# Slot counts of the experts in a two-layer backbone with routed experts: 44 and 44 quarters become 43 and 41

## The chip, the cores and the metric

The kernel runs on one core of a Trainium2 chip. The metric is the device time of one execution in microseconds (us). TensorE (PE) multiplies, VectorE (DVE) and ScalarE (ACT) work on its results, GpSimd (POOL) issues the gathers and stores of the expert layers, and SyncE (SP) issues the loads of weights. All transfers run on the core's 16 DMA engines.

## The reference, cut to what matters

512 tokens of width 1024 pass two layers. Each layer has a mixer (windowed attention in the first, a gated MLP over chunks in the second), a layer norm, and a mixture of 16 experts of which each token uses two; then another layer norm. All is float32.

```
def routed_moe(h, router_w, router_bias, w1, w3, w2):
    s = sigmoid(h @ router_w); s_sel = s + router_bias
    # of 4 groups of 4 experts the best group, of it the best two experts
    gate = sc / sum(sc)
    # for each expert, for its tokens:
    y = (silu(x @ w1[e]) * (x @ w3[e])) @ w2[e]
    out[token] += gate * y
```

An expert's w1 and w3 are 1024 x 512 each, its w2 is 512 x 1024. The number of tokens that an expert gets follows from the data: 1024 choices are spread over 16 experts.

## The kernel before, in words

**Slots.** The number of rows for an expert is fixed when the program is built. `VIS` (L29) lists for each layer 16 visits in the order in which they are done, as (rank, slots). Rank 0 is the expert that got the most tokens, 13 the one that got the fewest, among experts 0 to 13; experts 14 and 15 have rank -1 and come first, because their weights can be loaded before the routing is known. A token beyond the slots of its expert goes to a block for overflow (`more`), which runs only where a count needs it. Slots come in quarters of 32 rows. The first layer has 44 quarters, the second too.

**Units and groups.** `units_of` (L38) lays the visits' slots one behind the other in rows, in groups of 128 rows, and cuts them into units of 128, 64 or 32 rows that don't cross a group's edge. A layer has 11 groups: the rows of a group are gathered together from `hdr` by one indirect transfer on POOL's queue (`gather`, L994) and transposed on PE (`to_xT`, L1003). The list of a group's tokens comes from one-hot rows that DVE makes, one operation for each visit in the group and each of four blocks of tokens (`slots`, L977), and small matmuls (`tokens`, L960). The lists of group 0 and of groups 1 to 3 are made before the loop, those of the others in it.

**A unit's work.** `gemm1` (L1029) multiplies the unit's rows with w1 and w3: 8 weights of 128x1024, for 64 and 32 rows in 2 and 4 parts that lie side by side in the array. `glu` (L1040) is one operation on ACT and one on DVE, `to_hT` (L1049) transposes on PE and copies on ACT, `gemm2` (L1062) multiplies with 4 weights, `store` (L1072) scales on DVE and writes to `ydr` on POOL's queue, one transfer for 128 rows, two for 64, four for 32. In the loop of `moe` (from L1162) the second product of a unit comes after the first product of the next one. A float32 matmul stands as two instructions in the trace.

**Weights.** Each visit needs 12 pieces of 512 KB, all visits of a layer but the first two 168. `moe_pieces` (L162) puts them in order: eight for a visit's first product, and a visit's last four behind the first eight of the next, where it has one unit. SP issues them (L221) into a ring of tiles in a pool of 28 slots (NS); a piece that takes the slot of an older one waits until the last unit of that visit has used it. The expert of rank 0 in the second layer has 320 slots, in five units before the change, and holds its weights until the fifth.

**The end of a layer.** The last two units stay on the chip; the results of the others are gathered from `ydr` (`collect`, L1101), for which POOL waits until the last store has landed, and added to x on DVE (L1114). `last_norm` (L674) multiplies the last two units with their one-hot rows (L688), adds them (L696) and norms.

The order on each engine is set by a scheduler at build time, from the program's order and its dependencies.

Of the kernel before, what the change touches and what calls it, by code (L numbers as in the profile page):

```python
# [18 lines left out]
D = 1024  # L19
T = 512  # L20
NT = 4
E = 16
# [3 lines left out]
LOOK = 25  # L26


VIS = ([(-1, 64), (-1, 64), (4, 96), (0, 128), (8, 64), (5, 96), (6, 96), (9, 64), (7, 96), (1, 128), (10, 64), (11, 64),  # L29
# [3 lines left out]

NOV = 10
NR = E - 2
# [1 line left out]

def units_of(l):  # L38

    r, row = [], NOV * 128  # L40
    for v, (_, cap) in enumerate(VIS[l]):
        o = 0
        while o < cap:
            left = min(cap - o, 128 - row % 128)
            n = max(m for m in (128, 64, 32) if m <= left)
            r.append((v, o, n, row))
            o, row = o + n, row + n
    assert row % 128 == 0 and [u[2] for u in r[-2:]] == [64, 64]
    return r, row


UNITS = [units_of(l)[0] for l in range(2)]

ZR = [units_of(l)[1] - 128 for l in range(2)]


# [4 lines left out]
def make_consts():  # L61
# [26 lines left out]
    for l in range(2):  # L88
# [3 lines left out]
        cap, base = np.zeros(E), np.zeros(E)  # L92
        for v, (r, n) in enumerate(VIS[l]):
            k = NR + v if r < 0 else r
# [7 lines left out]
def hybrid_kernel(ctx: ExitStack, tc: tile.TileContext, A, out):  # L102
    nc = tc.nc
    V, SC, PE, GP, SP = nc.vector, nc.scalar, nc.tensor, nc.gpsimd, nc.sync
# [14 lines left out]
    def slot(shape, dt=F32, nm="s"):  # L119
        return S.tile(shape, dt, name=f"{nm}{nid()}", tag="s")  # L120
# [25 lines left out]
    def tt2(shape, dt=F32, nm="t"):  # L146
        return sm.tile(shape, dt, name=f"{nm}_{nid()}", tag="t2", bufs=9)
# [43 lines left out]
    def issue(n):  # L191
        while issued[0] < min(n, limit[0]):
            p = pieces[issued[0]]
            if p[0] == "moe" and p[2] > 1:
                raws[p] = slot([128, 1024], F32, "ring")
                fetch(p[1], VIS[p[1]][p[2]][0], p[3], raws[p])
                issued[0] += 1
# [18 lines left out]
    def fetch(l, r, j, t):  # L216

        if (l, r) not in regs:
            regs[l, r] = nc.values_load(RT[l]["int"][0:1, r:r + 1], engines=[mybir.EngineType.SP], min_val=0,
                                        max_val=E - 1, skip_runtime_bounds_check_because=why)  # L220
        SP.dma_start(t, A["moe"][l, bass.ds(regs[l, r], 1), j].rearrange("a p n -> (a p) n"))  # L221
# [40 lines left out]
    zero = cst.tile([128, 128], F32, name="zero")  # L262
# [55 lines left out]
    ydr = dr.tile([max(ZR) + 1, D], F32, name="ydr")  # L318
    for z in ZR:
        SP.dma_start(ydr[z:z + 1, :].rearrange("o (a b) -> (o a) b", b=128), zero[0:8, :])  # L320

# [428 lines left out]
    NG = [ZR[l] // 128 + 1 - NOV for l in range(2)]  # L750
# [100 lines left out]
    def plan(l):  # L851
# [86 lines left out]
        def gates():  # L938
# [14 lines left out]
            for u in range(2):  # L953
                q = tt2([128, 4, NR], F32, "pq")
                r = VIS[l][u - 2][0]
                V.tensor_tensor(q, g[:, :, :NR], pm[:, None, r, :].to_broadcast([128, 4, NR]), op=OP.mult)
# [3 lines left out]
    def tokens(gi, hot, n):  # L960

        p = psB()
        for i in range(n):
            for t in range(4):
                oh = small([128, 128], BF, "oh", 6)
                hot(oh, i, t)
                PE.matmul(p[:, i * 4:i * 4 + 4], oh, aux[:, t, :], start=(i == 0 and t == 0), stop=(t == 3),
                          skip_group_check=True)
        r = small([128, NOV, 4], F32, "sr")[:, :n]
        V.tensor_copy(r.rearrange("p a b -> p (a b)"), p[:, :n * 4])  # L970
        ix = small([128, NOV], F32, "six")[:, :n]
        iv = small([128, NOV], F32, "siv")[:, :n]
        V.scalar_tensor_tensor(ix, r[:, :, 1], 128.0, r[:, :, 0], op0=OP.mult, op1=OP.add)
        V.tensor_scalar(iv, r[:, :, 2], -OOB, OOB, op0=OP.mult, op1=OP.add)
        return V.tensor_add(gi, ix, iv)

    def slots(l, g0, g1):  # L977
        R = RT[l]

        def hot(oh, i, t):  # L980
            r0 = (NOV + g0 + i) * 128
            for v, (r, cap) in enumerate(VIS[l]):
                a = next(row for w, o, n, row in UNITS[l] if w == v)
                c0, c1 = max(a, r0), min(a + cap, r0 + 128)
                if c0 < c1:
                    k = R["key"][:, t, NR + v:NR + v + 1] if r < 0 else R["kr"][:, t, r:r + 1]
                    V.tensor_scalar(oh[:, c0 - r0:c1 - r0], iotab[:, :c1 - c0], k, -float(c0 - a), op0=OP.subtract,
                                    op1=OP.is_equal)
        return tokens(R["gi"][:, g0:g1], hot, g1 - g0)
# [39 lines left out]
    def gemm1(n, xt, c, get, adv):  # L1029
        p = psA() if n == 128 else psB()  # L1030
        to = parts(n, p)
        for k in range(8):
            w = get(k).rearrange("p (m h c) -> p h m c", m=2, h=len(to))
            for h, o in enumerate(to):
                PE.matmul(o.rearrange("p (m c) -> p m c", m=2), xt[:, k, c:c + n], w[:, h], start=(k == 0), stop=(k == 7),  # L1035
                          skip_group_check=True)
            adv()
        return p if n == 128 else p[:, :n * 8]
# [42 lines left out]
    def last_slots(l):  # L1081
# [5 lines left out]
        for u in range(2):  # L1087
            pt = psT()
            k = VIS[l][u - 2][0]
            for t in range(4):  # L1090
# [25 lines left out]
    def moe(l, rest, X):  # L1116
        R = RT[l]
        gfr = mdr[l * 4 + 3:l * 4 + 4, :]
        gf = {128: load_row(gfr, alloc=xslot)}
        gs = xslot([128, 768], F32, "gfs")  # L1120
        gf[64], gf[32] = gs[:, :512], gs[:, 512:]
        for n in (64, 32):
            for h in range(128 // n):
                SC.dma_start(gf[n][h * n:h * n + n, :], gfr[:, h * n * 8:(h + 1) * n * 8].to_broadcast([n, n * 8]))
        xg = {}
        slots(l, 0, 1)
        xg[0] = gather(R["gi"][:, 0:1])
        places, rows, gates = plan(l)
        places()
        listed = slots(l, 1, 4)  # L1130
        for g in (1, 2):
            xg[g] = gather(R["gi"][:, g:g + 1])
        first = pos["moe", l, 0, 0]
        limit[0] = len(pieces) if l else pos["ws",]
        done = [0]
        units = UNITS[l]
        n = len(units)
        more(l, gf)
        xt = {0: to_xT(l, xg[0])}
        pend = None  # L1140

        def stage(i):
            v = units[i][0]
            lastuse = i + 1 == n or units[i + 1][0] != v

            def adv():
                if lastuse:
                    done[0] += 1
                    issue(first + done[0] + LOOK)
            return lambda j: raw("moe", l, v, j), adv  # L1150

        def fin():
            i, ht = pend
            py = gemm2(units[i][2], ht, *stage(i))
            if i < n - 2:
                store(units[i][2], units[i][3], py, gf)
            elif i == n - 2:
                R["yp"] = slot([128, 512], F32, "ys")
                V.scalar_tensor_tensor(R["yp"], py, R["gs"][:, 0:1], gf[64], op0=OP.mult, op1=OP.mult)
            return py  # L1160

        for i, (v, o, m, row) in enumerate(units):  # L1162
            g, c = row // 128 - NOV, row % 128
            p = gemm1(m, xt[g], c, *stage(i))
            s = glu(m, p)
            if i == 0:
                with tc.issue_after(rows().ins):
                    rest(0, 4)
            if c == 0 and 2 < g + 2 < NG[l]:
                xg[g + 2] = gather(R["gi"][:, g + 2:g + 3])  # L1170
            if c + m == 128 and g + 1 < NG[l]:
                if g:
                    xt[g + 1] = to_xT(l, xg[g + 1])
                else:
                    with tc.issue_after(listed.ins):
                        xt[g + 1] = to_xT(l, xg[g + 1])
                if g and g + 3 < NG[l]:
                    slots(l, g + 3, g + 4)
            if i == n // 2:
                gates()  # L1180
            if i == n - 4:
                last_slots(l)
            if pend:
                fin()
            if i == n - 2:
                collect(l, 1, uslot)
                collect(l, 0, slot)
            if i == n - 1:
                combine(l, 1, X)
            pend = (i, to_hT(m, s))  # L1190
        py = fin()
        combine(l, 0, X)
        limit[0] = len(pieces) if l else pos["moe", 1, 2, 0]
        return py, gf[64]
# [188 lines left out]
    p = psA()  # L1383
# [9 lines left out]
    for f in range(8):  # L1393
        wh, wl = hl("winu", f)
        p = psB()
# [10 lines left out]
        p = psT()  # L1406
# [83 lines left out]
```

## Time and profile before

| what | value |
|---|---|
| median of 3 runs | 1202.01 us (1195.79 to 1202.34) |
| profiled execution | 1199.04 us, span 1197.3 us |
| PE busy | 1032.2 us, 86% |
| DVE, ACT, POOL busy | 614.7, 360.4, 264.4 us |
| DMA | 330.98 MB, 276 GB/s on the mean |
| first expert layer, PE | about 391 to 652 us |
| second expert layer, PE | about 889 to 1157 us |

The profile is of one execution. Times in the trace count from the start of its span, which is 1.7 us shorter than the execution. A busy PE is one with matmuls in its pipeline; the ends of matmuls are modelled, so that a row's start is surer than its end.

### The profile page before, as it was taken

To read this page: it belongs to the slowest core of one execution; us is meant where nothing else is said; L and a number is where in the kernel's file an instruction comes from. 1 tells how busy PE (TensorE), PEld (TensorE's weight loads), DVE (VectorE), ACT (ScalarE), POOL (GpSimd) and SP (SyncE) were. 2 spreads that over 40 slices of the span, in tenths; PEclk is the share of its full clock that TensorE was granted. 3 is DMA by queue.
4 is the path that set the end of the run, shared out by engine and by line. 5 is a ranking of instruction groups with operands and counts; after the bars stand their busy time and mean duration, and the time that the engine had idled before them with its cause. 6 is when DMAs were issued, how large, how long until landed. Compare 5 with 4: busy or idle time off the path is not lost. (4 is left out here: it accounts for less than half of the span.)

```text
span 1197.3 us, 17660 instructions
## 1 busy us (share of the span) xinstructions
PE 1032.2 (86%) x6216; PEld 588.8 (49%) x6216; DVE 614.7 (51%) x1532; ACT 360.4 (30%) x726; POOL 264.4 (22%) x245
## 2 busy tenths in 40 slices
PE   6789899996992999999999499699749999999980
PEld 2567665553782344444443277588623444433430
DVE  1798999785357621211113987875655211221137
ACT  1553487775312111111111443451211111111103
POOL 0153343323000123231003253300010222211131
PEclk9898999997996999999999699799869999999995
DMA  9935457447274999999998126466559994999981
GB/s 341 404 138 183 151 207 245 167 148 250 90 264 171 372 406 390 410 410 409 410 408 314 78 105 212 141 214 222 211 189 411 410 410 172 377 410 409 410 317 70
DMA packets 103673, 330.98 MB, mean 276 GB/s; under 512 B 13057, under 2 KB 23761, under 8 KB 103570
## 3 DMA queue, kind: packets, MB, share of 16 engines
q1 hardware_dynamic: 88336, 287.43, 63.0%
q0 software_dynamic: 10512, 27.28, 6.0%
q10 hardware_dynamic: 4722, 14.98, 3.5%
q8 instruction: 54, 0.88, 0.3%
q14 instruction: 49, 0.40, 0.1%
HBM read 310.72 MB, written 22.07 MB: 278 GB/s over the span
## 5 line engine op out<-in xcount | busy, mean ns | idle before, releaser
L1035 PE MATMUL pb<-ring,xt 128*32 128x256 f32 (+1 forms) x1824 | 221.7, 461 | 0.3 <-DMA ring<-in_moe 0.2
L1035 PEld LDWEIGHTS pb<-ring,xt 128*32 128x32 f32 (+1 forms) x1824 | 81.6, 120 | 114.5 <-issue 80.7
L1079 POOL DMA_DIRECT2D ydr<-ys x114 | 58.3, 517 | 320.9 <-DVE ys L1074 240.0
L1046 DVE TENSOR_TENSOR si<-si,pb 128x256 f32<-128x256 f32 (+1 forms) x43 | 15.6, 364 | 219.8 <-ACT si L1045 219.8
L363 POOL TENSOR_TENSOR raw<-raw,row 128x1024 f32<-128x1024 f32 x32 | 92.3, 2896 | 131.0 <-DMA raw<-in_mt 93.4
L1068 PE MATMUL pb<-ring,hh 128*32 128x256 f32 (+1 forms) x912 | 116.0, 462 | 0.7 <-issue 0.5
L361 DVE SCALAR_TENSOR_TENSOR raw<-raw,row 128x1024 f32<-128x1024 f32 x48 | 85.4, 1797 | 3.5 <-DMA row<-mdr 3.5
L1045 ACT ACTIVATE si<-pb 128x256 f32<-128x256 f32 (+1 forms) x43 | 14.6, 340 | 215.6 <-PE pb L1035 215.6
L1035 PE MATMUL pa<-ring,xt 128*128 128x512 f32 x160 | 72.7, 600 | 0.0
L1068 PEld LDWEIGHTS pb<-ring,hh 128*32 128x32 f32 (+1 forms) x912 | 40.0, 119 | 60.2 <-issue 44.4
L1057 ACT COPY hh<-pt 128x256 f32<-128x256 f32 (+2 forms) x48 | 17.1, 355 | 152.0 <-PE pt L1055 152.0
L998 POOL DMA_INDIRECT xg<-hdr,Rgi x22 | 23.6, 1071 | 174.2 <-DVE pq L900 85.4
L227 DVE TENSOR_TENSOR wl<-raw,wh 128x1024 fp32r<-128x1024 f32 x44 | 54.6, 1268 | 13.6 <-ACT wh L226 13.6
L562 DVE TENSOR_SCALAR_CACHE_REDUCE P<-pa,nsink 128x512 f32<-128x512 f32 (+1 forms) x64 | 50.5, 809 | 19.8 <-PE pa L558 9.8
L1074 DVE TENSOR_TENSOR ys<-pb,gfs 128x512 f32<-128x512 f32 (+1 forms) x39 | 22.1, 567 | 65.1 <-PE pb L1068 65.0
L564 ACT ACTIVATE P<-P,nm 128x512 f32<-128x512 f32 (+1 forms) x64 | 49.4, 774 | 11.9 <-DVE P L562 11.6
L598 ACT COPY PT<-pt 128x512 f32<-128x512 f32 x72 | 39.5, 581 | 28.7 <-PE pt L597 28.6
L226 ACT CAST wh<-raw 128x1024 fp32r<-128x1024 f32 x44 | 44.4, 1043 | 11.3 <-DMA mdr<-gr 5.4
L597 PE MATMUL pt<-cc,P 128*128 128x128 f32 x288 | 44.1, 282 | 4.1 <-ACT PT L598 3.5
L1035 PEld LDWEIGHTS pa<-ring,xt 128*128 128x128 f32 x160 | 29.1, 190 | 37.7 <-issue 36.2
L597 PEld LDWEIGHTS pt<-cc,P 128*128 128x128 f32 x288 | 31.2, 142 | 31.7 <-issue 25.8
L1015 ACT ACTIVATE xt<-pt,bc,gc 128x128 f32<-128x128 f32 x88 | 33.1, 456 | 32.9 <-PE pt L1009 26.3
(367 smaller groups left out, 2032.2 us busy)
## 6 DMA issues: line engine op xcount, KB each, us to landing
ring<-in_moe SPq DMA_DIRECT2D x336, 512.0 KB
raw<-in_mt SPq DMA_DIRECT2D x80, 512.0 KB
raw<-in_moe SPq DMA_DIRECT2D x48, 512.0 KB
raw<-in_mod SPq DMA_DIRECT2D x16, 512.0 KB
raw<-in_qkv SPq DMA_DIRECT2D x12, 512.0 KB
ydr<-ys POOLq DMA_DIRECT2D x42, 128.0 KB, 5.4
ydr<-zero SPq DMA_DIRECT2D x10, 512.0 KB
raw<-in_wo SPq DMA_DIRECT2D x8, 512.0 KB
```

What stands on the lines that cost most here:

```text
L226: SC.copy(hi, src)
L227: V.tensor_sub(lo, src, hi.bitcast(F32))
L361: V.scalar_tensor_tensor(w, w, 1.0, srow[0], op0=OP.mult, op1=OP.mult, accum_out=mv[l][:, j:j + 1])
L363: GP.tensor_mul(w, w, srow[0])
L562: V.tensor_scalar(P[j], reg, -0.125, nsink[:, p * 8 + j:p * 8 + j + 1], op0=OP.mult, op1=OP.min, accum_out=nm[:, j:j + 1])
L564: SC.activation(P[j], P[j], AF.Exp, bias=nm[:, j:j + 1], scale=-1.0, accum_out=sums[:, j:j + 1])
L597: PE.transpose(pt[:, j * 128:(j + 1) * 128], P[a * 4 + j][:, i * 128:(i + 1) * 128], idf)
L598: cp = SC.copy(tl[:, a, :], pt)
L1015: SC.activation(o, i, AF.Identity, bias=b, scale=g)
L1035: PE.matmul(o.rearrange("p (m c) -> p m c", m=2), xt[:, k, c:c + n], w[:, h], start=(k == 0), stop=(k == 7), skip_group_check=True)
L1068: PE.matmul(o, ht[f], w[:, h], start=(f == 0), stop=(f == 3), skip_group_check=True)
L1079: GP.dma_start(ydr[row:row + n, h * n * 8:(h + 1) * n * 8], ys[h * n:h * n + n, :])
```

## The change

Only the constants of the slots change, and what must follow from them.

- First layer: the expert of rank 13 gets 32 slots instead of 64 and moves up to the twelfth visit; ranks 11 and 12 are now the last two. 43 quarters. The units become 1 of 128 rows, 12 of 64 and 15 of 32 (3, 11 and 10 before), 28 instead of 24.
- Second layer: ranks 7, 12 and 13 get 32 slots instead of 64, the order is a new one, ranks 5 and 6 are last. 41 quarters. The units become 3 of 128 rows, 10 of 64 and 9 of 32 (2, 14 and 8 before), 22 instead of 24.
- The last two visits begin at a group's edge; the group ahead of them (group 9) may be part empty. It has 96 rows in the first layer and 32 in the second. Both layers keep 11 groups.
- The rows of `ydr` that no unit of the first layer writes, 32 of them, are set to zero by a transfer of 128 KB on SP's queue at the start; the empty end of a group's one-hot rows is set to zero on DVE.

```diff
-VIS = ([(-1, 64), (-1, 64), (4, 96), (0, 128), (8, 64), (5, 96), (6, 96), (9, 64), (7, 96), (1, 128), (10, 64), (11, 64),
-        (2, 128), (3, 128), (12, 64), (13, 64)],
-       [(-1, 64), (-1, 64), (8, 32), (2, 160), (3, 64), (9, 32), (0, 320), (10, 32), (4, 64), (5, 64), (6, 64), (1, 224),
-        (11, 32), (7, 64), (12, 64), (13, 64)])
+VIS = ([(-1, 64), (-1, 64), (4, 96), (0, 128), (8, 64), (5, 96), (6, 96), (9, 64), (7, 96), (1, 128), (10, 64), (13, 32),
+        (2, 128), (3, 128), (11, 64), (12, 64)],
+       [(-1, 64), (-1, 64), (7, 32), (8, 32), (2, 160), (9, 32), (3, 64), (0, 320), (10, 32), (11, 32), (4, 64), (1, 224),
+        (12, 32), (13, 32), (5, 64), (6, 64)])
...
     for v, (_, cap) in enumerate(VIS[l]):
         o = 0
+        if v == E - 2:
+            row += -row % 128
...
+    free = max(row + n for _, _, n, row in UNITS[0][:-2])
+    SP.dma_start(ydr[free:ZR[0], :].rearrange("p (a b) -> p a b", b=128),
+                 zero[:ZR[0] - free, None, :].to_broadcast([ZR[0] - free, D // 128, 128]))
...
         def hot(oh, i, t):
             r0 = (NOV + g0 + i) * 128
+            end = max(row + n for _, _, n, row in UNITS[l] if row < r0 + 128)
+            if end < r0 + 128:
+                V.memset(oh[:, end - r0:], 0.0)
...
             g, c = row // 128 - NOV, row % 128
+            whole = i + 1 == n or units[i + 1][3] // 128 != row // 128
...
-            if c + m == 128 and g + 1 < NG[l]:
+            if whole and g + 1 < NG[l]:
```

## Rows read from the trace of the kernel before

**Rows 1.** The page's slices: granted clock and DMA share in tenths, 40 slices.
```profile
PEclk9898999997996999999999699799869999999995
DMA  9935457447274999999998126466559994999981
```

**Rows 2.** Busy us by stretch (count) of each engine, granted clock, DMA share, GB/s.
```profile
412.50:651.50 239.00, 238.65 (x1720) 103.09 (x1720) 51.43 (x159) 34.35 (x87) 50.21 (x80) 1.00 1.00 396
910.90:1156.80 245.90, 243.64 (x1623) 97.15 (x1622) 49.99 (x168) 30.80 (x83) 49.23 (x77) 1.00 0.93 368
480.00:623.00 143.00, 142.68 (x879) 62.74 (x881) 28.23 (x103) 19.71 (x52) 26.10 (x41) 1.00 1.03 410
989.00:1018.00 29.00, 29.00 (x135) 12.09 (x137) 5.99 (x21) 3.46 (x9) 6.16 (x9) 1.00 0.42 160
```

**Rows 3.** Timeline of PE: start, us, engine, line, output and inputs, form, count.
```profile
557.42 7.13 PE L1068 MATMUL pa<-ring,hh 128*128 128x512 f32 x16
...
937.05 0.33 PE L1055 MATMUL pt<-cc,si 128*128 128x128 f32 x1
937.31 7.09 PE L1035 MATMUL pb<-ring,xt 128*64 128x512 f32 x32
944.33 1.93 PE L1068 MATMUL pb<-ring,hh 128*32 128x256 f32 x32
...
954.68 3.65 PE L1068 MATMUL pb<-ring,hh 128*64 128x512 f32 x16
958.26 0.44 PE L1055 MATMUL pt<-cc,si 128*128 128x128 f32 x2
958.63 3.66 PE L1035 MATMUL pb<-ring,xt 128*32 128x256 f32 x64
```

**Rows 4.** SP's queue: issues in four stretches, and the wait between the last two.
```profile
506.89 116.61 SPq L221 DMA_DIRECT2D ring<-in_moe  x84
887.12 102.98 SPq L221 DMA_DIRECT2D ring<-in_moe  x76
1017.52 5.95 SPq L221 DMA_DIRECT2D ring<-in_moe  x8
1017.52 121.97 SPq L221 DMA_DIRECT2D ring<-in_moe  x92
SPq L221 <- PE pt L1055: 26.9, 1, 26.9
```

**Rows 5.** Timeline of PE where the first expert layer ends.
```profile
646.19 5.37 PE L1068 MATMUL pb<-ring,hh 128*64 128x512 f32 x24
```

**Rows 6.** Timelines of PE, POOL and DVE where the second expert layer ends.
```profile
1156.78 0.70 PE L688 MATMUL pa<-ys,oT 64*128 64x512 f32 x2
1143.42 1.04 POOL L1079 DMA_DIRECT2D ydr<-ys  x2 [10.01 <-DVE ys L1074]
1150.37 1.08 POOL L1106 DMA_INDIRECT y<-ydr,prow  x1 [5.91 <-ACT si L1045]
1160.01 1.36 POOL L1106 DMA_INDIRECT y<-ydr,prow  x1 [0.30 <-issue]
1164.89 0.69 DVE L696 SCALAR_TENSOR_TENSOR x<-pa,x 128x512 f32<-128x512 f32 x1
```

**Rows 7.** Group of ACT, 32-row units: busy us, mean ns, idle before and its cause.
```profile
L1045 ACT ACTIVATE si<-pb 128x128 f32<-128x128 f32 x18 | 5.0, 278 | 59.3 <-PE pb L1035 59.3
```

**Rows 8.** Timeline of PE: the first ring unit, and the first of the 320-slot expert.
```profile
910.87 3.66 PE L1035 MATMUL pb<-ring,xt 128*32 128x256 f32 x64
966.07 7.09 PE L1035 MATMUL pb<-ring,xt 128*64 128x512 f32 x32
```

**Rows 9.** SP's issues among the first loads.
```profile
13.83 0.35 SPq L320 DMA_DIRECT2D ydr<-zero  x1
15.10 8.00 SPq L210 DMA_DIRECT2D raw<-in_mod  x6
```

**Rows 10.** Group of DVE: one-hot rows of 32 slots.
```profile
L987 DVE TENSOR_SCALAR oh<-iotab,pkr 128x32 bf16<-128x32 bf16 x40 | 8.9, 280 | 0.0
```

## The prediction

> **What bounds the kernel now.** I read the slices first: the two expert layers are the two long stretches in which the DMA digits stand at 9, and there the clock digits stand at 9 too [rows 1]. The table by stretch, cut to those two layers, shows TensorE (PE) busy for 238.65 of 239.0 us and 243.64 of 245.9 us at a granted clock of 1.00, its level of 2.4 GHz, while VectorE (DVE) needs 50 of them and ScalarE (ACT) 31 to 34 [rows 2]. In the same rows the DMA share is 1.00 and 0.93, at 410 GB/s where nothing holds it up. So two things run side by side at nearly the same length, PE work and the stream of weights, and the question for each layer is which of them ends last after the change. The prices of PE work come from its instructions in order of time [rows 3], the stream from the issues on SP's queue and what they waited for [rows 4].
>
> The stream now, layer by layer. In the first layer the last 84 weights are issued without a hole up to 623.5 us [rows 4]. A weight lands about 10 us behind its issue: after a hole the queue takes eight at once [rows 4] and then one each 1.27 us (an estimate from these). The last one is thus there by 634, and PE starts its last second matmul group near 648 (3.58 before 651.56) [rows 5]. Fourteen us of lead: PE is the bound. In the second layer 76 weights are issued in 103.0 us, then the queue stands for 26.9 us because a ring slot is not free, and the other 92 take 122.0 us, to 1139.5 [rows 4]. During the hole the DMA share is 0.42 over 29 us [rows 2]: 17 us of transfer lost. The slot belongs to the expert with 320 slots, whose weights are held until its last unit. The last weight lands near 1149.5, and PE's last group begins near 1153.2 (3.58 before 1156.78) [rows 6]. Only 4 us of lead: PE still ends last here, but barely.
>
> **PE work, part by part.** From one row's start to the next, or by a row's time less the 0.07 us by which it overlaps the next [rows 3]: a 64-row unit costs 7.02 + 3.58, and 0.37 for its transposes, 10.97 us. A 32-row unit costs 3.59 + 1.86 + 0.26, 5.71. A 128-row unit's second group takes 7.07, its first has twice the matmuls, 14.14, and with 0.6 it comes to 21.8. So 32 rows cost 5.71, 5.49 or 5.45 us by the size of the unit: the price goes by quarters, and small units pay little. First layer: the units go from 3, 11, 10 (of 128, 64, 32 rows) to 1, 12, 15: -43.6 + 10.97 + 28.55 = -4.1 us. Second layer: from 2, 14, 8 to 3, 10, 9: +21.8 - 43.9 + 5.7 = -16.4 us. Groups stay at 11 in each layer, so gathers and the transposes of a group stay.
>
> Four more units in the first layer also mean four more ACT and DVE steps; at 0.28 us for ACT's on a 32-row unit [rows 7] they lie under the 3.59 us of the next unit's first group, and its second group is only wanted after that. If that cover failed, some 1 us a unit would show; I keep 0.5 us in all, so the first layer is worth **-3.6** (bounds -4.1 and 0). Its lead of 14 us carries the whole gain.
>
> **The stream in the second layer.** Its bytes stay: 168 weights. Two things move. First, the start. From the first ring unit at 910.87 to the first unit of the 320-slot expert at 966.07 [rows 8] PE did 9 quarters, 6.1 us each with all that lies between. The new order puts 10 quarters there, but five experts instead of four: PE arrives at 972, and wants the 64th weight at about 978. That one is issued at 887.1 + 63 x 1.355 = 972.5 and lands near 983. PE must wait about 5 us; bounds 0 (the queue gets ahead) and 10 (a second expert late as well), I take 5.5 since the rate is measured in this stretch. Second, the hole. Now 84 weights instead of 76 go before it, the last issued at about 1001 and landing at 1011; the slot comes free two quarters earlier, plus the wait: 1017.5 - 10.9 + 5.5 = 1012. The queue hardly stands still. Then 84 weights at 1.326 (122.0 / 92) are 111.4 us, to 1123.5; the last unit of this expert now has 128 rows and frees a weight each 1.77 us instead of 0.45, so I add 6 us (bounds 0 and 12): last issue 1130, landing 1140. PE: 1156.8 - 16.4 + 5.5 = 1145.9. PE ends last, 10.9 us earlier: **-11** (bounds -17 with no wait, -4 where the stream ends as late as now).
>
> **The rest.** The new transfer of zeros takes one place in SP's queue among the first loads, which go out 1.27 us apart [rows 9], and PE's first products need those loads in turn: +0.6, bounds 0 and 1.3. In the second layer the lists of groups 1 to 3 are made of 7 pieces instead of 6, four more one-hot operations of 0.28 [rows 10], before PE's second group may start: +0.5, bounds 0 and 1.1. The other one-hot operations and the few memsets lie in the loop, where DVE is idle for four fifths of the time [rows 2]. The tail: the last unit that is stored sends its two stores at 1143.42, the gathers on POOL's queue run from 1150.37, the last from 1160.01, and the sums after PE's end start at 1164.89 [rows 6]. That unit now has 32 rows and four stores, 0.52 more each, ahead of the gathers: +1 if the store is last; if PE waits for weights at its end, the gathers are done under that wait and the tail shrinks by up to 6. I take 0.
>
> Sum: -3.6 - 11 + 0.6 + 0.5 = -13.5. The profiled execution took 1199.04 us; the runs shown have a median of 1202.01, 3 us above. That gives 1185.5 or 1188.5; as the two unsure terms, wait and tail, have more room downward, I take **1185**.
>
> **Rivals.** (a) The whole PE saving arrives: no wait at the start, and the tail shrinks: -20.5 - 4, about 1175. For it speaks that the hole disappears and the queue has 17 us to give back; against it that these come after the first 60 weights are late.
>
> (b) The stream is the floor: the second layer ends with its last weight, no more than the 4 us of lead are gained, and the first layer gives 3.6: -7.6 + 1, about 1194. It decides if the last issue stays near 1139. For it speaks the DMA share of 1.03 where no slot is missing [rows 2]; against it the hole of 17 us that the stream can use. The Trainium skill, page "DMA: Bandwidth & Descriptors", section "Bandwidth", puts what HBM gives one core at about 358 GB/s with both cores of a pair streaming; an estimate by that page is 246 us for the 88.1 MB of a layer's 168 weights, as long as the layer is now, so that nothing could be gained in either. If that bound held here, this rival would be certain; the trace disagrees, with 410 GB/s over 143 us [rows 2], and the measurement decides.
>
> (c) Slower: runs of one-quarter experts starve PE. Such an expert costs PE 5.71 us and the stream 12 x 1.33 = 15.9, a debt of 10.3. The second layer has four of them now and seven then, six of these in pairs: three more debts are +31, less 20.5 gives +10, 1209 to 1212. It decides if fewer than about 20 weights are ahead when a pair begins. Against it: two pairs follow right behind the 320-slot and the 224-slot expert, when the ring (28 slots) is full, and the first is the start that is priced above.
>
> (d) The slots don't hold the counts, and the block for overflow runs: 12 loads with nothing ahead, 16 us, 21.8 of PE and lists and a gather of some 10: about +48, 1240. The reference's router gives on its inputs, after ranking, 25 tokens to the expert that gets 32 slots in the first layer, and 27, 23, 21, 20, 14, 14, 6 to those that get 32 in the second (62 and 293 where the limits are 64 and 320): this does not happen unless the kernel routes otherwise.
>
> **How the numbers follow.** Forecast 0.56, its own range 1178 to 1193; (a) 0.15; (b) 0.19; (c) 0.07; (d) 0.02; 0.01 for others. The range of 8 in 10 leaves out (c) and (d) and the end of (a): 1174 to 1198. A measurement of this kernel can tell about 1% from no change, here 12 us. Faster than 1190: most of the forecast (0.50), (a), a tenth of it from (b): 0.67. Slower than 1214: (d) and part of (c): 0.05. The rest, 0.28, within.
>
> **What would show it.** Right: 11 groups as before, PE work of the first layer 3 to 4 us shorter with no wait for a weight; in the second, one wait of about 5 us for the weights of the 320-slot expert, the queue's stop of 26.9 us gone or under 10, and the last ring issue near 1130 minus 3 for the earlier start. Wrong: PE gaps behind the pairs of 32-slot experts, a last issue that has not moved, a longer idle time between PE's end and the last sums, or stages before and between the expert layers that change by more than 2 us, which nothing here explains.

## The result, and the profile after

The changed kernel takes 1186.9 us (median of four runs, 1184.33 to 1190.71) where the kernel before took 1199.58 beside it (four runs, 1195.79 to 1202.34): a ratio of 0.9898, interval [0.9861, 0.9936]. Forecast were 1185 and a range of 1174 to 1198. The profiled execution took 1186.24 us with a span of 1184.4; before it was 1199.04 and 1197.3. So the time is right. The sum behind it is not right in each term, as the length of each phase shows. A layer is counted from its first product to the first matmul of the row sums that follow.

```
us                                     before   after   difference
start to the first layer's products     391.4   386.8      -4.6
first expert layer                      260.1   260.6      +0.5   (forecast -3.6)
between the layers                      237.6   241.0      +3.4   (forecast +0.5 of it)
second expert layer                     267.7   255.5     -12.2   (forecast -11)
from there to the end of the span        40.5    40.6      +0.1   (forecast  0)
```

The second layer gave all of it. The first layer gave nothing, and the 4.6 us at the start are taken as scatter of single executions: in the eleven profiled executions of this study, one of each kernel, that stretch takes between 385.6 and 391.4 us, without a visible relation to the edits. The layers scatter less: five kernels with the second layer of the change have 254.5 to 255.5 us in it, two with the old one 267.5 and 267.7.

The slices of the page after, granted clock and DMA share in tenths, beside [rows 1]: the two stretches of 9 are still the two expert layers.

```profile
PEclk7799999998996999999999799799959999999995
DMA  9934457547274999999998316365449999898991
```

The same table as [rows 2] for the kernel after: busy us (count) by engine, then clock, DMA share and GB/s. The first two rows are the two layers from their first weights out of the ring on, the third is the stretch in which the ring's slots are short.

```profile
408.30:647.40 239.10, 237.97 (x2150) 103.27 (x2149) 51.52 (x178) 34.47 (x94) 60.68 (x100) 1.00 1.00 394
909.80:1143.80 234.00, 228.87 (x1570) 94.96 (x1569) 47.42 (x162) 29.40 (x79) 47.11 (x74) 1.00 0.98 386
...
1000.00:1035.00 35.00, 33.91 (x172) 15.82 (x172) 9.27 (x41) 5.65 (x13) 7.89 (x10) 1.00 0.85 331
```

The reader is to see two things. In the second layer PE has 228.87 us of work in 234.0, 14.8 us of work less than before, and the DMA share went up from 0.93 to 0.98. And where the DMA share fell to 0.42 for 29 us in [rows 2], it now falls to 0.85 for 35. In the first layer nothing moved.

SP's queue after: all issues of the second layer's weights as one row (start, us, count), those up to the first stop as another, and its longest waits on PE (us in total, times, longest).

```profile
886.86 244.67 SPq L224 DMA_DIRECT2D ring<-in_moe  x168
886.86 117.94 SPq L224 DMA_DIRECT2D ring<-in_moe  x88
```

```profile
SPq L224 <- PE pb L1045: 23.1, 30, 7.9
SPq L224 <- PE pa L1045: 13.2, 8, 5.0
...
SPq L224 <- PE pt L1065: 9.6, 2, 7.8
```

Against [rows 4] the single stop of 26.9 us is gone, and the last issue goes out at 1131.5 instead of 1139.5. In its place stand shorter stops, the longest of 7.9 us; the first comes after 88 weights, where it was 76 before and the forecast had 84 (one expert more ahead is 12 weights).

What the weight loads of PE waited for at the start of the second layer, first after (888 to 975 us), then before (889 to 966): us in total, times, longest.

```profile
PEld pb L1045 <- DMA ring<-in_moe: 6.7, 8, 1.1
...
PEld pb L1078 <- DMA ring<-in_moe: 1.3, 2, 1.0
```

```profile
PEld pb L1068 <- DMA ring<-in_moe: 1.4, 5, 0.3
...
PEld pb L1035 <- DMA ring<-in_moe: 1.1, 4, 0.3
```

That is 8.0 us after, 2.5 before: 5.5 us more waiting of the loads, the size that was forecast. Not all of it is PE's loss, since a load can wait while PE still works on the matmuls before. By starts, PE takes 65.1 us from its first ring unit (909.83) to the expert with 320 slots; before it took 55.2 [rows 8] with one 32-row unit less, which at the forecast's 5.71 leaves about 4 us (an estimate). The timeline of PE after shows where it lies (start, us, operation, count, wait before).

```profile
925.31 1.08 PE L1045 MATMUL pb<-ring,xt 128*64 128x512 f32 x4 [0.17 <-DMA ring<-in_moe]
926.65 1.08 PE L1045 MATMUL pb<-ring,xt 128*64 128x512 f32 x4 [0.26 <-DMA ring<-in_moe]
...
935.91 0.64 PE L1078 MATMUL pb<-ring,hh 128*32 128x256 f32 x8 [0.55 <-DMA ring<-in_moe]
...
974.92 1.08 PE L1045 MATMUL pb<-ring,xt 128*64 128x512 f32 x4
```

Four matmuls, a short wait, four matmuls: PE takes each weight as it lands. The 64-row matmuls are those of the expert with 160 slots, the third from the ring, the 32-row ones the second product of the expert before it. The expert with 320 slots begins at 974.92 (forecast 972) without a gap on PE.

### The profile page after: what moved, and what is told of

It reads as the page before. It is cut to its first block, busy times and chain, and to the rows that moved or that the text cites. A ratio compares the mean times of both kernels' runs of the same rounds, so it can differ in the third digit from the quotient of the medians.

```text
span 1184.4 us, 18461 instructions
## 1 busy us (share of the span) xinstructions
PE 1014.6 (86%) x6596; PEld 589.6 (50%) x6596; DVE 611.5 (52%) x1548; ACT 359.9 (30%) x730; POOL 271.2 (23%) x262
## 5 line engine op out<-in xcount | busy, mean ns | idle before, releaser
L1045 PE MATMUL pb<-ring,xt 128*32 128x256 f32 (+1 forms) x2112 | 228.1, 440 | 1.1 <-DMA ring<-in_moe 0.8
L1045 PEld LDWEIGHTS pb<-ring,xt 128*32 128x32 f32 (+1 forms) x2112 | 86.7, 117 | 114.9 <-issue 70.4
L1089 POOL DMA_DIRECT2D ydr<-ys x132 | 67.0, 513 | 319.2 <-DVE ys L1084 258.9
L1056 DVE TENSOR_TENSOR si<-si,pb 128x128 f32<-128x128 f32 (+1 forms) x46 | 16.1, 350 | 206.9 <-ACT si L1055 203.4
L1078 PE MATMUL pb<-ring,hh 128*32 128x256 f32 (+1 forms) x1056 | 119.5, 441 | 1.7 <-ACT hh L1067 0.8
L1055 ACT ACTIVATE si<-pb 128x128 f32<-128x128 f32 (+1 forms) x46 | 15.1, 329 | 219.4 <-PE pb L1045 219.4
L1084 DVE TENSOR_TENSOR ys<-pb,gfs 128x256 f32<-128x256 f32 (+1 forms) x42 | 22.6, 537 | 81.5 <-PE pb L1078 79.9
L1067 ACT COPY hh<-pt 128x128 f32<-128x128 f32 (+2 forms) x50 | 17.0, 339 | 146.1 <-PE pt L1065 139.4
L1045 PE MATMUL pa<-ring,xt 128*128 128x512 f32 x128 | 59.4, 604 | 0.6 <-DVE xt L1027 0.6
L1025 ACT ACTIVATE xt<-pt,bc,gc 128x128 f32<-128x128 f32 x88 | 33.1, 457 | 38.2 <-PE pt L1019 20.9
L614 PE MATMUL pb<-PT,Vt 128*64 128x512 f32 x144 | 38.8, 617 | 3.6 <-ACT PT L605 3.6
```

Source lines behind the costliest of these rows:

```text
L614: m.append(PE.matmul(po[a * 64:(a + 1) * 64, :], Vt[kb // 3][:, kb % 3, g * 64:(g + 1) * 64], tl[:, a, :], start=(i == 0), stop=(i == nb - ...
L1078: PE.matmul(o, ht[f], w[:, h], start=(f == 0), stop=(f == 3), skip_group_check=True)
L1089: GP.dma_start(ydr[row:row + n, h * n * 8:(h + 1) * n * 8], ys[h * n:h * n + n, :])
```

## The experiments

**The second layer's part alone.** The first layer's list of slots goes back to the old one, and with it the transfer of zeros.

```
-        ... (1, 128), (10, 64), (13, 32), (2, 128), (3, 128), (11, 64), (12, 64)],
+        ... (1, 128), (10, 64), (11, 64), (2, 128), (3, 128), (12, 64), (13, 64)],
...
-    SP.dma_start(ydr[free:ZR[0], :]..., zero...)
```

> Only the second layer has the new slots (41 quarters); the first keeps its 44, with its three 128-row units, and the transfer of zeros is gone since nothing is left empty there. Theory A (the whole gain is the second layer's, since in the first the two 128-row units that were lost cost as much as the quarter that was saved): second expert layer 255 to 257 us from first to last matmul instead of 267.7, first 260, execution 10 to 13 us under before, within 1.5 us of the full change. Theory B (both layers gain, as predicted, and something between them took the first one's part back): 3 to 4 us slower than the full change.

Measured: 1186.4 us against 1199.19, ratio 0.9906 [0.9882, 0.9929]; the second layer takes 254.6 us, the first 261.0. That is the whole gain of the change, as theory A had it.

**The first layer's part alone.** The second layer's list goes back.

```
-  (7, 32), (8, 32), (2, 160), (9, 32), (3, 64), (0, 320), (10, 32), (11, 32), (4, 64), (1, 224), (12, 32), (13, 32), (5, 64), (6, 64)
+  (8, 32), (2, 160), (3, 64), (9, 32), (0, 320), (10, 32), (4, 64), (5, 64), (6, 64), (1, 224), (11, 32), (7, 64), (12, 64), (13, 64)
```

> Only the first layer has the new slots (43 quarters, 28 units); the second keeps its 44. Theory A: the first expert layer takes 260 us as before, execution within 1.5 us of before. Theory B: 256 to 257 us in the layer and 3 to 4 us under before.

Measured: 1199.44 us, ratio 1.0009 [0.9994, 1.0025]; the first layer takes 261.6. That is theory A again: one quarter less of slots is worth nothing in the order in which the change puts it.

**The first layer with its wide units kept.** In the change the expert with 32 slots comes ahead of two experts with 128, which are then cut across groups into 32, 64 and 32 rows. Here it comes behind them.

```
-  (1, 128), (10, 64), (13, 32), (2, 128), (3, 128), (11, 64), (12, 64)
+  (1, 128), (2, 128), (3, 128), (10, 64), (13, 32), (11, 64), (12, 64)
```

> The full change, with the first layer's visits in another order: the three 128-slot experts side by side, then ranks 10 (64) and 13 (32), then ranks 11 and 12. Still 43 quarters, 11 groups and a part-empty group 9, but the three 128-row units stay whole: 3, 10 and 11 units instead of 1, 12 and 15. Theory A (price by the size of the units): the first expert layer falls to about 255 us (one 64-row unit of 10.9 becomes one 32-row unit of 5.8), execution 4 to 6 us under the full change. Theory B (price by quarters alone): the same as the full change within 1 us. If the weights of the four small visits at the end come late, PE waits for weights behind 600 us and some of the 5 us is lost.

Measured: 1179.36 us (1177.07 to 1183.4), ratio 0.9847 [0.9825, 0.9869]; the first layer takes 254.4 us, 6.2 less than after the change: theory A. The same 43 quarters, as 3 units of 128 rows, 10 of 64 and 11 of 32 instead of 1, 12 and 15.

**Small units only.** The first layer of the change, cut into units of 32 rows but for the last two visits (39 of 32, 2 of 64).

```
-            n = max(m for m in (128, 64, 32) if m <= left)
+            n = max(m for m in ((128, 64, 32) if l or v > E - 3 else (32,)) if m <= left)
```

> The full change, but the first layer is cut into 32-row units throughout, but for the last two visits: 39 units of 32 rows and 2 of 64. Theory A1 (what a 32-row unit costs too much comes from its matmuls being mixed with those of units of another width): without the mixture 32 rows cost 5.45 us of products, the products of the layer take 234 to 236 us, the layer 258 to 262. Theory A2 (a 32-row unit costs 5.66 us of products in any company): products 242, the layer 266 to 269.

Measured: 1186.06 us, ratio 0.9894 [0.9869, 0.9919]; the first layer takes 262.6 us, its products 237.6 (by starts, in a table further below). Both theories missed: A1 had 234 to 236 and 258 to 262, A2 242 and 266 to 269. The groups of PE by form in that layer (busy us, mean ns, idle before), ring weights alone:

```profile
L1045 PE MATMUL pb<-ring,xt 128*32 128x256 f32 x2240 | 131.5, 381 | 0.0
L1078 PE MATMUL pb<-ring,hh 128*32 128x256 f32 x1120 | 70.1, 380 | 0.0
```

2240 matmuls are 35 units, so a unit is busy for (131.5 + 70.1) / 35 = 5.76 us. With next to no change of width left, a 32-row unit costs what it costs in the mixed layers (5.71 before and 5.81 after, from the rows further below). So what the mixing adds is 0.1 us a unit at most, and the 5.45 of the forecast is not reached without it either.

**No wide units.** The first layer ordered as in the third experiment, its three 128-row units cut into six of 64.

```
-            n = max(m for m in (128, 64, 32) if m <= left)
+            n = max(m for m in ((128, 64, 32) if l else (64, 32)) if m <= left)
```

> l0_aligned with the first layer's three 128-row units cut into six of 64, in the same order of visits and weights. Theory A (price by the size of the units): a 128-row unit's products take 20.9 us and two 64-row units' 21.9, with three transposes' hand-overs more: the first layer 3 to 5 us longer than l0_aligned's 254.4. Theory B (the gain of l0_aligned comes from the order of its visits, the units cost alike by quarters): the same layer time within 1 us.

Measured: 1185.62 us, ratio 0.9887 [0.9856, 0.9917]; the first layer takes 257.8 us, 3.4 more than with the wide units, as theory A had it. The medians are 6.3 us apart; of the 9.3 us between the two profiled executions 5.8 lie at the start (391.4 against 385.6 us), which scatters by itself. PE's busy time in the first layer, with the three wide units and then without (first number the stretch, then its length and PE's busy us):

```profile
385.60:640.00 254.40, 252.47 (x1857) 113.95 (x1857) 61.64 (x196) 39.68 (x99) 54.44 (x85) 1.00 1.02 402
```

```profile
391.40:649.20 257.80, 256.26 (x2000) 105.67 (x1999) 62.53 (x202) 40.85 (x105) 58.21 (x93) 1.00 1.01 395
```

The 3.4 us are PE work (252.47 to 256.26), not waiting, and the clock is 1.00 in both.

**New counts in the old order.** The second layer has the 41 quarters of the change, in the order of before as far as they allow: ranks 5 and 6 stand last as in the change, and so ranks 11, 12 and 13, with 32 slots each, stand in a row. The units are 2 of 128 rows, 11 of 64 and 11 of 32.

```
-  (7, 32), (8, 32), (2, 160), (9, 32), (3, 64), (0, 320), (10, 32), (11, 32), (4, 64), (1, 224), (12, 32), (13, 32), (5, 64), (6, 64)
+  (8, 32), (2, 160), (3, 64), (9, 32), (0, 320), (10, 32), (4, 64), (7, 32), (1, 224), (11, 32), (12, 32), (13, 32), (5, 64), (6, 64)
```

> The full change, but the second layer's 41 quarters stand in the order of before as far as they can: ranks 8, 2, 3, 9, 0, 10, 4, then 7 with 32 slots, 1, 11, 12 and 13 with 32, then 5 and 6. Nine quarters instead of ten ahead of the 320-slot expert. Theory S (the stream of weights is the floor where the order leaves the hole in it): SP's queue stands for 20 us or more at that expert, the last weight is issued near 1137 to 1141, PE waits for weights 10 us or more behind it, the second layer takes 261 to 266 us and the execution is 6 to 11 us over the full change. Theory P (PE work alone): the layer takes 255 to 257, execution within 2 us of the full change.

Measured: 1201.95 us against 1197.95, ratio 1.0027 [1.001, 1.0044]; the second layer takes 272.3 us, longer than before the change and 6 us more than even theory S had. SP's issues of that layer, its longest wait on a transpose, and PE's waits for weights over the layer:

```profile
883.88 252.53 SPq L224 DMA_DIRECT2D ring<-in_moe  x168
```

```profile
SPq L224 <- PE pt L1065: 29.4, 5, 28.3
```

```profile
PEld pb L1078 <- DMA ring<-in_moe: 16.6, 13, 3.3
...
PEld pb L1045 <- DMA ring<-in_moe: 16.0, 17, 1.8
```

The queue stops for 28.3 us (26.9 before), its issues take 252.5 us (252.4 before), and PE, with less work, only waits longer for its weights: 32.6 us. Less work by itself makes this layer no shorter.

Why it even grows stands at its end. The layer ends 21.6 us behind the last issue at 1136.4; before it was 17.3. First the issues from 1135 to 1136 (count, size, us to landing), then the stretch from 1144 on:

```profile
ring<-in_moe SPq DMA_DIRECT2D x1, 512.0 KB, 18.8
y<-ydr,prow POOLq DMA_INDIRECT x2, 8.5
```

```profile
1144.00:1158.00 14.00, 8.41 (x20) 1.21 (x16) 0.75 (x1) 0.00 (x0) 0.12 (x1) 0.56 0.91 363
```

The gathers of the results run beside the last weights, and a weight lands 18.8 us behind its issue, where the last ones of the next experiment take 10.7. While PE waits for them, its granted clock falls to 0.56 (near the level of 1.2 GHz), and four matmuls that took 1.08 us take 1.98. No run moved the gathers, so their part is not measured by itself.

**Old counts in the new order.** The converse: three experts keep 64 slots (44 quarters in all).

```
-  (7, 32), ... (12, 32), (13, 32), (5, 64), (6, 64)
+  (7, 64), ... (12, 64), (13, 64), (5, 64), (6, 64)
```

> The full change, but in the second layer ranks 7, 12 and 13 keep their 64 slots, in the new order of visits: 44 quarters, 4, 9 and 10 units. With l1_old_order it completes the square of counts and order. Theory J (joint: the stream and PE are nearly equally long, so that either edit alone leaves the other limit): the layer takes 264 to 271 us, execution within 6 us of before. Theory O (the order alone brings the gain, because the hole in the stream is what matters): 255 to 259 us, execution 8 to 12 us under before.

Measured: 1196.84 us against 1199.05, ratio 0.9977 [0.996, 0.9994]; the second layer takes 266.5 us, as theory J had it. PE's waits for weights fall to 4.4 us and the queue's longest wait to 18.7, and PE is busy for 262.85 of 266.0 us:

```profile
SPq L224 <- PE pb L1045: 32.1, 28, 18.7
```

```profile
888.00:1154.00 266.00, 262.85 (x1761) 110.79 (x1760) 61.04 (x201) 35.83 (x93) 54.06 (x83) 0.99 0.95 374
```

This closes a square of kernels. Second layer in us: old counts, old order 267.7; new counts, old order 272.3; old counts, new order 266.5; both 255.5. Neither half by itself shortens the layer by more than 1.2 us. The square is not quite pure: the order also changes how visits are cut into units (2, 14, 8; 2, 11, 11; 4, 9, 10; 3, 10, 9), and the old order could only be kept in part.

**The 160-slot expert first.** Wide units kept in the first layer; in the second the expert that waited goes to the front, so that the stream gets ahead.

```
-  (7, 32), (8, 32), (2, 160), (9, 32), (3, 64), (0, 320), ...
+  (2, 160), (7, 32), (8, 32), (9, 32), (3, 64), (0, 320), ...
```

> The first layer as in l0_aligned; in the second the 160-slot expert is first and the experts of ranks 7, 8, 9 follow, so that its slots begin a group: 4, 8 and 9 units instead of 3, 10 and 9. Theory P: 1 to 2 us less PE work, execution 1 to 2 us under l0_aligned. Theory S: the first expert holds its 12 weights for five quarters, the queue stops there early and the three small ones behind it starve PE: waits for weights of 10 us or more before 1000 us, the layer 262 to 266 us, execution 7 to 11 us over l0_aligned.

Measured: 1182.45 us, ratio 0.9863 [0.9832, 0.9893]; the second layer takes 257.3 us, between what the two theories gave, so that both missed (by the time too: 3.1 us over the kernel with the wide units kept). Three 32-slot experts in a row now follow the big one, and PE's waits for weights over the layer are no smaller than after the change:

```profile
PEld pb L1078 <- DMA ring<-in_moe: 6.8, 9, 1.5
...
PEld pb L1045 <- DMA ring<-in_moe: 5.1, 7, 1.1
```

The lead did not last: the wait only moved.

**Both layers in another order.** The first layer with all four 128-slot experts kept whole; in the second no two 32-slot experts stand side by side until the 320-slot one has been passed, and the 160-slot expert stands late.

```
+  first:  (4, 96), (5, 96), (11, 64), (9, 64), (10, 64), (3, 128), (0, 128), (1, 128), (2, 128), (13, 32), (6, 96), (7, 96), (8, 64), (12, 64)
+  second: (12, 32), (5, 64), (11, 32), (0, 320), (10, 32), (13, 32), (4, 64), (1, 224), (8, 32), (9, 32), (2, 160), (7, 32), (6, 64), (3, 64)
```

> The counts of the full change in orders chosen for both limits. First layer: 4 units of 128, 11 of 64, 5 of 32, by the prices measured 232 us of products and 8 units less than in the full change: 251 to 253 us. Second layer: the 320-slot expert after three small visits (four quarters), then small and large ones in turn, the 160-slot one late: the queue stops for about 16 us early and makes up for it, PE hardly waits: 247 to 251 us. Execution 1169 to 1175 us. If the hole in the stream decides instead, the second layer stays at 255 or more and the execution at 1178 or more.

Measured: 1171.71 us (1169.81 to 1174.9, six runs) against 1197.95, ratio 0.9773 [0.9748, 0.9797]: faster than the kernel before and, by the two medians, than the changed one. The first layer takes 255.7 us, more than expected. The second takes 247.5 by the count used so far, but here that count ends too early: the scheduler put the first row sums ahead of the last second product.

```profile
1129.13 1.99 PE L695 MATMUL pa<-ys,oT 64*128 64x512 f32 x8 [0.48 <-DVE ys L1169]
1130.95 1.02 PE L695 MATMUL pt<-ys,oT 64*128 64x512 f32 x2
1131.90 3.65 PE L1078 MATMUL pb<-ring,hh 128*64 128x512 f32 x16
```

The last product ends near 1135.5. Without the 2.8 us of row sums the layer takes 251.1 us, just over the 247 to 251 that were expected, and 4.4 less than after the change. SP's issues, PE's waits for weights, and the layer up to the last issue:

```profile
879.49 238.20 SPq L224 DMA_DIRECT2D ring<-in_moe  x168
```

```profile
PEld pb L1045 <- DMA ring<-in_moe: 3.9, 9, 0.8
```

```profile
880.00:1118.00 238.00, 233.66 (x1552) 98.78 (x1552) 58.71 (x200) 33.63 (x87) 41.26 (x65) 0.99 1.01 396
```

With a DMA share of 1.01 the DMA engines hardly stand still any more, and PE hardly waits. The end of the span, 44.0 us by the same count and so 3.4 longer than after the change, holds that last product.

## Why the prediction was right, and where it was not

**The second layer: right.** Forecast was -11, as -16.4 of PE work and +5.5 of early wait; measured -12.2. The two terms can be told apart only roughly: PE's busy time fell by 14.8 us and its idle time grew by 2.9 (2.3 to 5.1, from the first ring unit on); by starts the early wait is about 4. The steps that were to show it came: the stop of 26.9 us is gone, no stop is over 10, the last issue is at 1131.5 where 1127 to 1130 were foretold. The 6 us that the forecast added for the slots of the 320-slot expert came as a DMA share of 0.85 over 35 us, 5 us of transfer lost. One place was wrong: the early wait falls on the 160-slot expert, some 40 to 50 us sooner than on the 320-slot one. The forecast followed PE only to the expert whose weights are many, and took the queue's mean rate of 1.355 us a weight; yet two 32-slot experts open the layer, and the third already waits. That the size came out although the place was wrong is in part luck. So is that the 84 weights before the first stop, which were 88, did no harm.

**That the gain needs both halves** was not said, though the forecast's own question, which of the two ends last, holds it. The square shows it: in the old order the stream takes 252.4 and 252.5 us, whatever PE's work, and with the old counts PE is busy for nearly the whole layer in the new order too (262.85 of 266.0 us). Rival (c), small experts that starve PE, is seen in the old order: of the 32.6 us of waits 8.3 lie where three 32-slot experts stand in a row (1090 to 1125 us) and 21.1 behind them, in the last two visits, where weights also land late.

**The first layer: the step that failed.** Forecast -3.6, measured +0.5 here and no gain with that half alone. Waiting took little of it: PE's busy time in the layer is 258.61 us before and 258.30 after, its idle time grew from 1.5 to 2.3. The step was "the price goes by quarters, and small units pay little". The groups of PE by form in that layer, first before, then after (ring weights alone; busy us, mean ns, idle before):

```profile
L1035 PE MATMUL pb<-ring,xt 128*64 128x512 f32 x288 | 66.0, 597 | 0.1
L1035 PE MATMUL pa<-ring,xt 128*128 128x512 f32 x96 | 42.6, 596 | 0.0
L1035 PE MATMUL pb<-ring,xt 128*32 128x256 f32 x640 | 36.6, 381 | 0.0
L1068 PE MATMUL pb<-ring,hh 128*64 128x512 f32 x144 | 33.1, 598 | 0.3 <-DVE sr L970 0.3
L1068 PE MATMUL pa<-ring,hh 128*128 128x512 f32 x48 | 21.4, 598 | 0.0
L1068 PE MATMUL pb<-ring,hh 128*32 128x256 f32 x320 | 20.5, 382 | 0.0
```

```profile
L1045 PE MATMUL pb<-ring,xt 128*64 128x512 f32 x320 | 73.4, 596 | 0.0
L1045 PE MATMUL pb<-ring,xt 128*32 128x256 f32 x960 | 56.1, 381 | 0.0
L1078 PE MATMUL pb<-ring,hh 128*64 128x512 f32 x160 | 38.0, 600 | 0.5 <-ACT hh L1067 0.5
L1078 PE MATMUL pb<-ring,hh 128*32 128x256 f32 x480 | 31.0, 382 | 0.0
...
L1045 PE MATMUL pa<-ring,xt 128*128 128x512 f32 x32 | 14.1, 595 | 0.0
...
L1078 PE MATMUL pa<-ring,hh 128*128 128x512 f32 x16 | 7.1, 599 | 0.0
```

The counts are those of the forecast: 640 to 960 matmuls are five more units of 32 rows, 288 to 320 one more of 64, 96 to 32 two less of 128. The times are not. (56.1 + 31.0 - 36.6 - 20.5) is 30.0 us for the five, where the forecast's 5.45 of products makes 27.3. These rows count the overlap at each start of a run twice. Without it, with every matmul counted from its start to the next start on PE, waits included, the first layer divides as follows (units in brackets):

```
us              128 rows    64 rows       32 rows      transposes  other   layer
before          62.6 (3)   120.3 (11)    55.4 (10)        7.9       14.0    260.1
after           20.9 (1)   131.6 (12)    84.9 (15)        8.9       14.3    260.6
l0_aligned      62.1 (3)   108.6 (10)    62.0 (11)        7.7       14.0    254.4
aligned_no128     -        172.8 (16)    62.2 (11)        8.6       14.2    257.8
l0_all32          -         21.2 (2)    216.4 (39)       11.4       13.6    262.6
```

(The last three lines are the third, fifth and fourth experiment.) A unit costs 20.7 to 20.9, 10.6 to 11.0 and 5.5 to 5.7 us by its size, and 5.2, 5.4 and 5.6 us for each 32 rows; the forecast had 5.3, 5.3 and 5.45. It had read each price inside one unbroken run of a unit [rows 3]; in the layer the runs are broken by other units' transposes, and each run is handed over to the next. That this makes the difference is argued, not shown; the wide unit came out cheaper than its run. The change trades two wide units for six small ones: -41.7 + 11.3 + 29.5 of products is -0.9 instead of -4.6, four more sets of transposes take 1.0 (forecast 0.5), the rest 0.3. That is the missing 4 us. That the cut into units makes it is shown by the two kernels that keep the wide units (6.2 us less) and that cut them in the same order (3.4 more, of which 2.3 are products and 0.9 transposes).

What makes the small ones dearer is settled only in part. The Trainium skill, page "TensorEngine Tiling (Array Packing)", section "Key Properties", says that a change of the tiling mode drains the engine. The trace shows little of it: a 32-row unit costs 5.55 us where nearly all units have that width, and 5.54 to 5.66 where widths alternate. The rest goes with the unit, whatever stands beside it; why stays open.

**The small terms.** From the start of the route's last matmul to the second layer's first product it takes 25.0 us instead of 24.5, against +0.5 forecast for the lists; but four other kernels with the same second layer take 24.2 to 25.5, so that this can't be told. Nor can the transfer of zeros (+0.6): the first products that wait for the early loads end at 31.5 us before and 33.1 after the change, at 33.1 too in the kernel that lacks the transfer, and at 32.1 in the other half, which has it. The end kept its length, as forecast. The bound "stages that change by more than 2 us" was broken by the start, which is taken as scatter, and by the 3.4 us between the layers, where 1.7 us lie between the end of the first layer and the first transposes of the next mixer, a part that had not been priced. Four kernels with the changed first layer have 25.7 to 27.1 us in that part, two with the old one 24.9 and 25.4; the reason was not pursued.

**Rivals.** The second layer of (a), with the whole saving of PE's work, came only with the other order (251.1 us, 16.6 less than before). (b), the stream as floor, did not hold: 168 weights, 88.1 MB, went out in 244.7 us after the change and in 238.2 in the best order, at 396 GB/s. The Trainium skill, page "DMA: Bandwidth & Descriptors", section "Bandwidth", puts what HBM gives one core at about 358 GB/s where both of a pair stream. With one core at work here the trace stays above that, as in [rows 2]. (d) did not occur: the result has no time near 1240.

So the time was right for its largest term, and within 2 us of the median, but partly by luck: the first layer's 4 us were missing, the second layer gave 1 us more than forecast, the 1.1 us of small terms can't be seen, and the rest lies within the scatter of the runs (1184.33 to 1190.71 us).

## What to carry to other kernels

Where work and the stream that feeds it are nearly of one length, count the saving of neither alone: make the square of both edits before believing a sum. Order the users of a stream by what each lends it (much work for its bytes) and borrows (little work), for the order decided here whether the saved work arrived (255.5 us) or not (272.3). Take the price of a small unit of work from the sum over a stage, from one start to the next, and not from inside its longest unbroken run; a cut that saves rows but breaks wide units may give all of it back.

## What was not expected of the hardware

A price that differs by a few per cent by the shape of the work decided a whole term: 128 rows as one unit took 20.7 us, as two of 64 rows 21.4 (six units for 64.2 us, 172.8 less 108.6), at the same clock of 1.00 and with the weights on hand. A weight that landed 10.7 us behind its issue in one kernel took 18.8 in another, where gathers ran beside it at the end of a layer. And eleven kernels that are nearly alike up to there start their first expert layer anywhere between 385.6 and 391.4 us, so that single profiles of this kernel are better compared by stage than by their span.
